# Where matmul operands start: on-chip tiles moved to multiples of 64 and 512 bytes in a fused mixer and FFN block

## The chip, the cores and the metric

The kernel runs on 1 core of one Trainium2 chip. The metric is device time in microseconds (us): the median of repeated executions of the whole program, and for the profile the span from the first to the last instruction of one profiled execution. TensorE (PE) multiplies, VectorE (DVE) and ScalarE (ACT) work on elements, GpSimd (POOL) fills and issues some of the DMAs, SyncE (SP) issues the others. The memory on the core that the engines read has 128 partitions; every tile occupies the same byte range of each partition, and in this text "start" is the byte at which that range begins.

## What is computed

One layer of a block over 1024 tokens of width 1024, all in float32:

```
h = rmsnorm(x);  proj = h @ w_in                      # 5128 columns
q, k, v, f_logit, g_b, g_c, hc, gate_conv, gate_attn = split(proj)
ya = g_b * causal_conv3(g_c * hc)                      # 512 channels, 3 taps
yb = softmax(q k^T / 8 + cumulated log f, causal) v    # 8 heads of 64
merged = sigmoid(gate_conv) * (ya @ w_branch[0]) + sigmoid(gate_attn) * (yb @ w_branch[1])
x = x + rmsnorm(merged @ w_out)
h = rmsnorm(x);  g, u = split(h @ w_gate_up)           # 2816 columns each
x = x + rmsnorm((silu(g) * u) @ w_down)
```

The convolution adds, for each channel, three neighbours in time: `w[2]*z[s] + w[1]*z[s-1] + w[0]*z[s-2]`, with zeros ahead of the first token.

## The kernel before

**Products.** A float32 factor is split into a high and a low part (`split`, L120: a rounding copy on ACT into a tile of type float32r, a subtraction on DVE), and each product is three matmuls (`mm3`, L125): high by high, high by low, low by high. Nearly all of them have 512 columns of the moving tile, 2048 bytes per partition, against a weight tile of 128 columns, 512 bytes. The large products run by a Strassen scheme of seven products of 512 by 512 by 128 in place of eight (`strassen`, L509; `prod`, L485, four times `mm3`).

**Stages, in order.** (1) The first norm, transposes of x against the identity `ident`, and v with the forget logits (`v_tile`, L342): 8 row tiles, each 8 k by 2 halves of 260 columns by 3 matmuls into `pv`, 384 in all; the moving tiles are v's weights `wvh` and `wvl`, [128, 8, 520]. (2) 18 pairs of column blocks of w_in for q and k, the convolution's inputs and the gates: 18 x 7 x 12 = 1512 matmuls into `b1` to `b3`, and `ma`, `mb` for the last pair. The convolution is here: kind "z" (L860) writes the product of two blocks into `zt`, kind "gb" (L866) takes the three taps on DVE. (3) Attention: scores `sp` (pairs of matmuls of 64 rows), transposes `tps`, values `po` in plain float32, and between them the convolution's branch `pba`, 192 matmuls in all. (4) The attention's branch, `pbb`: 192. (5) The output projection `pm`, 384, with the two norms. (6) FFN gate and up, 22 column blocks: 22 x 7 x 12 = 1848, into `b1` to `b3`; the first product of blocks 0 to 6 is made ahead (`f_first`, L1260) while the last rows are normed. (7) The down products `pd`: 7 x 11 x 4 x 3 = 924 (`product`, L1483), then the last norm.

Where `strict` names engines, they keep the order written; elsewhere the order of PE's work is that of the program's scheduler. DMAs are issued by SP (weights, x) and POOL (stores of intermediate results).

**Where tiles lie.** A pool is a stack of tiles that grows from the low end of the memory (left) or from the high end (right); a tile takes its size rounded up to 32 bytes. The left side begins with 1152 bytes of the framework, which is 18 x 64. Then come the constants (L150 to L160): `ident`, `tri`, `ones` and `mask` of 512 bytes, `cw` of 48 (takes 64), `bf` of 32, `ff` of 256, together 2400. So the first pool after them starts at 3552 = 55 x 64 + 32, and since the tiles there are multiples of 64, every tile of the pool `w` (`raw`, `hi`, `lo`, `sx`, `s4`, `s4h`, `s4l`: all weight tiles of stages 2 to 7, and moving tiles of the scores and of `pd`) starts 32 bytes past a multiple of 64; so do `pt`, `ptT`, `yh`, `yl`, `hah`, `hal`, `hch`, `hcl`, `ghi` and `glo` behind it. The right side ends at 229376 = 3584 x 64; the small tiles of `stat` take 1440 bytes, the two tiles of `z` 4128 each (1026 columns are 4104 bytes), so the first tile of `z` starts at 219680 = 3432 x 64 + 32, and below it, in whole multiples of 64, lie `hB11` to `hB22`, `hT12`, `hT34`, `woh`, `wol`, `hth` and `htl`, again 32 past. Exceptions are the second tile of `z` (which serves once as `wbl` and once as `v0`), some of the six `vf` tiles of 2080 bytes, and `ident`: they start at multiples of 64. In `wvh`, 32 past as well, row k starts at 2080 k and its second half 1040 later, so the halves of successive k start 32, 48, 0 and 16 past a multiple of 64. In bytes modulo 512 the places are 480 in the pool `w`, and for `hah`, `hal`, `hch` and `hcl`; 352 for `ptT`, `yh` and `yl`, 160 for `ghi` and `glo`, and 32 for the right side.

The convolution's tile has 1026 columns: two zeros, filled by POOL, and 1024 values, so that each tap reads 512 columns at an offset of 0, 1 or 2.

Of the kernel before, what the change touches and what calls it, by code (L numbers as in the profile page):

```python
# [10 lines left out]
F32 = mybir.dt.float32  # L11
F32R = mybir.dt.float32r
AF = mybir.ActivationFunctionType
ALU = mybir.AluOpType
# [3 lines left out]
P = 128  # L18
S = 1024
D = 1024  # L20
KT = D // P
ST = S // P
NC = 512
H = 8
# [10 lines left out]
C_GB, C_GC, C_HC = 1544, 2056, 2568  # L35
C_GATE_C, C_GATE_A = 3080, 4104
VF = AW + H
TAIL = 4
NPRE = 7

# [5 lines left out]
def block_kernel(  # L46
# [16 lines left out]
    n1, n2 = slice(0, NC), slice(NC, S)  # L63
# [3 lines left out]
    class InOrder:  # L67
# [15 lines left out]
    nc = SimpleNamespace(  # L83
        **{e: InOrder(e) for e in engines}
    )
# [19 lines left out]
    def f32(ap):  # L105
        return ap.bitcast(F32)
# [4 lines left out]
    def sub(o, a, b):  # L111
        nc.vector.tensor_tensor(o, a, b, op=ALU.subtract)

    def mul(o, a, b):
        nc.vector.tensor_tensor(o, a, b, op=ALU.mult)

    def copy(o, a):
        nc.scalar.activation(o, a, AF.Copy)
# [13 lines left out]

    cpool, _ = pool("const")
    stat, _ = pool("stat", 4, side="right")
    dpool, _ = pool("dram", space=DRAM)

    c_dram = dpool.tile([H, S], F32, name="c_dram")
# [9 lines left out]
    ri_dram = [dpool.tile([2, S], F32, name=f"ri_dram{j}") for j in range(4)]  # L147
    sg_dram = [dpool.tile([2, P, S], F32, name=f"sg_dram{d}") for d in range(8)]

    ident = cpool.tile([P, P], F32, name="ident")  # L150
    make_identity(bass_nc, ident)
    tri = cpool.tile([P, P], F32, name="tri")
# [1 line left out]
    ones = cpool.tile([P, P], F32, name="ones")  # L154
    nc.vector.memset(ones, 1.0)
    mask = cpool.tile([P, P], F32, name="mask")
    cw = cpool.tile([P, 3, 4], F32, name="cw")
    bf = cpool.tile([P, H], F32, name="bf")
    nc.gpsimd.dma_start(bf, b_f[0].partition_broadcast(P))
    ff = cpool.tile([P, ST, H], F32, name="ff")  # L160

    def bcast_row(row, p, **kw):
        g = p.tile([P, row.shape[-1]], F32, **kw)
# [27 lines left out]
    zp, z_close = pool("z", side="right")  # L191

    def z_tile(name, dt=F32, w=S):
        return zp.tile([P, S + 2], dt, tag="z", name=name, bufs=2)[:, :w]

    h_pool, h_close = pool("h1", side="right")
    def h_pair(name, shape):
# [6 lines left out]
    hB22 = h_pair("hB22", [P, 4, NC])  # L204
    ax, ax_close = pool("ax", side="right")
    ap, ap_close = pool("a")
    av, av_close = pool("av")
    psa, psa_close = pool("psa", 4, space=PSUM)

# [5 lines left out]
    wrs = []  # L215

    def vf_tile(tag="vf", dt=F32):
        return ap.tile([P, VF], dt, tag=tag, name=tag, bufs=6)

    def load_wv():  # L220
        k = len(wrs)
        wr = ax.tile([P, VF], F32, tag="wr", name="wr", bufs=4) if k < 4 else vf_tile()
        nc.sync.dma_start(wr, win[k * P : (k + 1) * P, C_V : C_V + VF])
        wrs.append(wr)
# [10 lines left out]
    xq.append(load_x(2))  # L235
    warm = st_tile("warm")
    nc.scalar.activation(warm, ones[:, 0:1], AF.Sqrt)
    wvh = av.tile([P, KT, VF], F32R, name="wvh")
    wvl = av.tile([P, KT, VF], F32R, name="wvl")
    gm = ax.tile([P, D], F32, name="gm")  # L240


# [12 lines left out]
    turns(14)  # L255

    def split_wv(k, halves="hl"):
        if "h" in halves:
            copy(wvh[:, k, :], wrs[k])
        if "l" in halves:  # L260
            sub(wvl[:, k, :], wrs[k], f32(wvh[:, k, :]))

    def norm_sum(st):

# [76 lines left out]

    def v_tile(st, ops):  # L342
        pv = psa.tile([P, 2, NC], F32, tag="pv", name="pv", bufs=2)
        hv = VF // 2
        for k in range(KT):
            src = ops[k // 4]
            for n in range(2):
                cs = slice(n * hv, (n + 1) * hv)
                mm3(
                    pv[:, n, :hv],  # L350
                    (src[0][:, k % 4, :], src[1][:, k % 4, :]),
                    (wvh[:, k, cs], wvl[:, k, cs]),
                    k == 0,
                    k == KT - 1,
                )
        vs = av.tile([P, VF], F32, tag="vs", name="vs", bufs=2)
        copy(vs.rearrange("p (n c) -> p n c", n=2), pv[:, :, :hv])
        nc.gpsimd.dma_start(v_dram[st * P : (st + 1) * P, :], vs[:, :AW])
        add(ff[:, st, :], vs[:, AW:VF], bf)

# [186 lines left out]
    t0_, t0_close = pool("att0")  # L547
# [67 lines left out]
    cbs, qks, stacks, vs_, rsums = {}, {}, {}, {}, {}  # L615
# [150 lines left out]
    def step_qk(t):  # L766
        j, rows_ = steps[t]
        if j not in rsums:
            rsums[j] = t0_.tile([P, 2 * ST], F32, tag="rsum", name="rsum", bufs=2)
        for i in rows_:  # L770
            sps[t, i] = qk(j, i)

# [53 lines left out]
    for ij, (kind, j, _, _) in enumerate(jobs):  # L826
        if ij == 2:
            logf_pre = forget_sums()
        if ij == 4:
            forget_store(*logf_pre)  # L830
        if ij < 2:
            if ij == 0:
                heads = [
                    prep_first(wcols(a), t) for (_, _, a, _), t in zip(jobs, ((r0, h0, l0), None))
                ]
                firsts = [strassen_first(w, h1b, psm, pp) for w, _ in heads]
            (w, r1), (c11, p1) = heads[ij], firsts[ij]
            w = {**w, **prep_rest(wcols(jobs[ij][3]), r1)}
            if ij == 1:
                pairs.q.append(pairs.prep(*pairs.srcs.popleft()))  # L840
            _, c12, c21, c22 = strassen(w, h1b, psm, pp, p1)
        elif ij < len(jobs) - 1:
            if ij == 12:
                k_load(0)
                q_load(0)
                cb_of(0, 0)
                cb_of(0, 1)
            c11, c12, c21, c22 = strassen(pairs.get(), h1b, psm, pp)
        else:
            w = pairs.get()  # L850
            psm_close()
            strict[0] = engines
            pss, pss_close = pool("pss", space=PSUM)
            c11, c12, c21, c22 = last_pair(w)
        if kind == "qk":
            so = pp.tile([P, NC], F32, tag="so", name="so")
            copy(so, c11)
            for r, c, t in ((0, n1, so), (0, n2, c12), (1, n1, c21), (1, n2, c22)):
                nc.gpsimd.dma_start(qk_dram[j][r, :, c], t)
        elif kind == "z":  # L860
            zt = z_tile("zt", w=S + 2)
            nc.gpsimd.memset(zt[:, 0:2], 0.0)
            mul(zt[:, 2 : 2 + NC], c21, c11)
            mul(zt[:, 2 + NC : 2 + S], c12, c22)
            zts[j] = zt
        elif kind == "gb":  # L866
            for m, parts in ((j, (c11, c12)), (j + 1, (c21, c22))):
                zt = zts.pop(m)
                for n in range(2):
                    o = n * NC  # L870
                    ot = pp.tile([P, NC], F32, tag="so", name="ot")
                    nc.vector.tensor_scalar(
                        ot, zt[:, o + 2 : o + 2 + NC], cw[:, 2, m : m + 1], None, op0=ALU.mult
                    )
                    for t in (1, 0):
                        nc.vector.scalar_tensor_tensor(
                            ot, zt[:, o + t : o + t + NC], cw[:, t, m : m + 1], ot,
                            op0=ALU.mult, op1=ALU.add,
                        )
                    mul(ot, ot, parts[n])  # L880
                    nc.gpsimd.dma_start(ya_dram[m][:, o : o + NC], ot)
        else:
            so = c11
            strict[0] = ()
            if ij < len(jobs) - 1:
                so = pp.tile([P, NC], F32, tag="so", name="so")
                nc.scalar.activation(so, c11, AF.Sigmoid)
                for t in (c12, c21, c22):
                    nc.scalar.activation(t, t, AF.Sigmoid)
            for r, c, t in ((0, n1, so), (0, n2, c12), (1, n1, c21), (1, n2, c22)):  # L890
                nc.gpsimd.dma_start(sg_dram[j][r, :, c], t)
# [280 lines left out]
    for n in range(2):  # L1172
        ns = slice(n * NC, (n + 1) * NC)
        for d in range(KT):
# [14 lines left out]
            if n == 0:  # L1189
                wr = flat(raw_t())  # L1190
# [185 lines left out]
    count = {"raw": 0, "ops": 1}  # L1376
    SETS = TAIL

# [127 lines left out]
    p1, c22, c11, c12 = (quarter(s_) for s_ in (4, 6, 0, 2))  # L1506

    def wide(name, w=4):
        return gp.tile([P, w], F32, name=name)

    sums = {n: wide(f"sum_{n}") for n in ("c11", "c12", "c22", "c21", "both", "rest")}

    def sq_scale(o, c, key, sl):

# [59 lines left out]
    product(xb, False, to(c22, add, c22, xb), between=rows_0)  # L1574
    product(xb, False, last, TAIL, rows_1)
    gp_close()
# [38 lines left out]
```

## Time and profile before

| what | value |
|---|---|
| time, median of 3 runs | 1361.17 us (1360.53 to 1362.53) |
| the profiled execution: span | 1362.4 us (its own time is not given apart from the span) |
| granted TensorE clock, mean | 0.998 |
| instructions | 17714 |
| DMA | 186.36 MB, 137 GB/s on average |

The page gives the busy time of each engine and its share of the span. Busy time of PE counts from a matmul's start to its modelled end, and matmuls overlap in the pipeline, so how fast PE goes is read from the distance between the starts of successive matmuls: in the list of instructions in order of time, or from a run of matmuls in the chain of waits, its length divided by its count. PEld is the loading of a matmul's weights, which runs beside the matmul before it. All matmuls stand at line 75 of the kernel, a helper that issues every instruction; they are told apart by the names of their tiles, written as out<-moving,weights, with buffer numbers left out (`b` for `b1` to `b3`).

### The profile page before, as it was taken

The numbers are of one execution on the slowest core, as the hardware profiler recorded it, in microseconds if no ns is written. First come the engines' busy times: TensorE is split into PE (matmuls) and PEld (weight loads), VectorE is DVE, ScalarE is ACT, GpSimd is POOL, SyncE is SP. The second block draws the span as 40 slices with busy tenths as digits, with TensorE's granted clock in tenths as the row PEclk, the third lists the DMA queues.
The fourth block names the chain that finished last, engine by engine and source line by source line (L and its number), as shares of the span: only waits on it lengthen the run. The fifth ranks groups of instructions, "written<-read, shape, count | busy, mean of one in ns | idle before, by whom it ended". The sixth has DMA issues, their size and how long they took to land.

```text
span 1362.4 us, 17714 instructions
## 1 busy us (share of the span) xinstructions
PE 1341.2 (98%) x6753; PEld 1099.8 (81%) x6753; DVE 933.0 (68%) x1445; ACT 535.5 (39%) x851; POOL 128.0 (9%) x256
## 2 busy tenths in 40 slices
PE   9999999999999999999999999999999999999997
PEld 7978888888887878788887788888888888888886
DVE  6974767754446766765668698676677766676585
ACT  6642222243345756514446232223222323444452
POOL 0001000010112212000002121100111011000000
PEclk9999999999999999999999999999999999999999
DMA  5432422333325545362235565322333236976441
GB/s 187 117 108 85 125 70 85 102 117 106 99 92 173 156 140 187 114 204 80 90 110 179 162 200 161 101 94 84 116 101 116 86 116 227 355 239 199 161 162 63
DMA packets 153256, 186.36 MB, mean 137 GB/s; under 512 B 9409, under 2 KB 106753, under 8 KB 153170
## 3 DMA queue, kind: packets, MB, share of 16 engines
q1 hardware_dynamic: 138434, 136.67, 32.5%
q0 software_dynamic: 14736, 48.54, 9.7%
q8 instruction: 53, 0.87, 0.3%
q14 instruction: 33, 0.27, 0.1%
HBM read 136.10 MB, written 49.09 MB: 136 GB/s over the span
## 4 chain that ended last, share of the span: by engine, by line
PE 58%; DVE 2%; issue 1%; DMA 1%; ACT 1%; POOL 0%; DVEq 0%; POOLq 0%; ACTq 0%
PE b L75 28%; PE pd L75 16%; PE pm L75 5%; PE pbb L75 3%; PE pba L75 2%; PE po L75 1%; PE tps L75 1%; PE sp L75 1%; DMA pre_dram<-s 1%; DVE tt L75 0%; DMA pre_dram<-c 0%; PE tp L75 0%; ACT tt L75 0%; DVE lo L75 0%; DMA raw<-in_w_gate_up_dram 0%
## 5 line engine op out<-in xcount | busy, mean ns | idle before, releaser
L75 DVE TENSOR_TENSOR c<-c,b 128x512 f32<-128x512 f32 x195 | 133.1, 683 | 93.2 <-PE b L75 68.3
L75 DVE TENSOR_TENSOR lo<-raw,hi 128x1024 fp32r<-128x1024 f32 (+1 forms) x93 | 112.1, 1205 | 86.0 <-PE b L75 71.5
L75 ACT ACTIVATE hi<-raw 128x1024 fp32r<-128x1024 f32 (+1 forms) x100 | 101.7, 1018 | 130.4 <-PE b L75 81.2
L75 PE MATMUL b<-hth,hi 128*128 128x512 f32 x352 | 139.1, 395 | 0.1
L75 PE MATMUL b<-hth,lo 128*128 128x512 f32 x352 | 138.1, 392 | 0.0
L75 PE MATMUL b<-htl,hi 128*128 128x512 f32 x352 | 137.2, 390 | 0.0
L75 ACT ACTIVATE hi<-sx 128x1024 fp32r<-128x1024 f32 x41 | 43.5, 1061 | 222.7 <-PE b L75 197.1
L75 PEld LDWEIGHTS b<-hth,lo 128*128 128x128 f32 x352 | 66.0, 188 | 15.6
L75 PEld LDWEIGHTS b<-hth,hi 128*128 128x128 f32 x352 | 66.1, 188 | 14.8 <-DVE c L75 1.0
L75 PEld LDWEIGHTS b<-htl,hi 128*128 128x128 f32 x352 | 66.1, 188 | 14.6
L75 DVE TENSOR_TENSOR lo<-sx,hi 128x1024 fp32r<-128x1024 f32 x41 | 50.2, 1225 | 34.6 <-PE b L75 30.8
L75 PE MATMUL b<-hah,hi 128*128 128x512 f32 x176 | 70.5, 403 | 2.1 <-ACT c L75 2.1
L75 DVE TENSOR_TENSOR sx<-raw 128x512 f32<-128x512 f32 x78 | 53.7, 688 | 23.4 <-DMA raw<-in_w_in_dram 11.7
L75 PE MATMUL b<-hah,lo 128*128 128x512 f32 x176 | 69.4, 395 | 0.0
L75 PE MATMUL b<-hal,hi 128*128 128x512 f32 x176 | 69.1, 393 | 0.0
L75 PE MATMUL pd<-hi,lo 128*128 128x512 f32 x160 | 62.6, 391 | 0.0
L75 PE MATMUL pd<-hi 128*128 128x512 f32 x160 | 62.3, 392 | 0.0
L75 PE MATMUL pd<-glo,ghi 128*128 128x512 f32 x148 | 57.7, 390 | 0.0
L75 PE MATMUL pd<-ghi 128*128 128x512 f32 x148 | 57.7, 390 | 0.0
L75 PE MATMUL pd<-ghi,glo 128*128 128x512 f32 x148 | 57.6, 389 | 0.0
L75 PE MATMUL b<-hT34h,lo 128*128 128x512 f32 x136 | 53.4, 393 | 0.0
L75 PE MATMUL b<-hT34h,hi 128*128 128x512 f32 x136 | 53.0, 390 | 0.4 <-DVE c L75 0.4
(369 smaller groups left out, 3367.8 us busy)
## 6 DMA issues: line engine op xcount, KB each, us to landing
raw<-in_w_gate_up_dram SPq DMA_DIRECT2D x51, 512.0 KB, 4.0
raw<-in_w_in_dram SPq DMA_DIRECT2D x35, 512.0 KB, 4.2
a_dramS<-um POOLq DMA_DIRECT2D x44, 256.0 KB, 3.1
a_dramA<-um POOLq DMA_DIRECT2D x33, 256.0 KB, 3.0
xt<-in_x_dram SPq DMA_DIRECT2D x16, 512.0 KB, 4.3
sg<-sg_dram SPq DMA_DIRECT2D x32, 256.0 KB, 4.1
graw<-a_dramS SPq DMA_DIRECT2D x14, 512.0 KB, 4.0
sg_dram<-c POOLq DMA_DIRECT2D x24, 256.0 KB, 2.3
```

What stands on the lines that cost most here:

```text
L75: ins = getattr(self.engine, name)(*args, **kw)
```

## The change

It alters where tiles start, and the shape of three tiles. The constants `cw`, `bf` and `ff` come first, with `cw` and `bf` taking 64 bytes each; empty tiles named "pad" are put into the pools `stat`, `a` and `g`; `vf`, `vs` and `rsum` get longer rows; `wvh` and `wvl` hold each half of 260 columns in a row of 272; `zt` has 1024 columns and no zeros, and the taps that would read before the first token leave out the first one or two columns of the first half. Everything computed stays the same.

```diff
+HV = VF // 2
     stat, _ = pool("stat", 4, side="right")
+    stat.tile([P, 24], F32, name="pad", bufs=1)
...
+    cw = cpool.tile([P, 4, 4], F32, name="cw")[:, :3, :]
+    bf = cpool.tile([P, 2 * H], F32, name="bf")[:, :H]
+    ff = cpool.tile([P, ST, H], F32, name="ff")
     ident = cpool.tile([P, P], F32, name="ident")
...
     mask = cpool.tile([P, P], F32, name="mask")
-    cw = cpool.tile([P, 3, 4], F32, name="cw")
-    bf = cpool.tile([P, H], F32, name="bf")
     nc.gpsimd.dma_start(bf, b_f[0].partition_broadcast(P))
-    ff = cpool.tile([P, ST, H], F32, name="ff")
...
-        return zp.tile([P, S + 2], dt, tag="z", name=name, bufs=2)[:, :w]
+        return zp.tile([P, S], dt, tag="z", name=name, bufs=2)[:, :w]
...
     ap, ap_close = pool("a")
+    ap.tile([P, 32], F32, name="pad")
...
-        return ap.tile([P, VF], dt, tag=tag, name=tag, bufs=6)
+        return ap.tile([P, VF + 8], dt, tag=tag, name=tag, bufs=6)[:, :VF]
...
-    wvh = av.tile([P, KT, VF], F32R, name="wvh")
-    wvl = av.tile([P, KT, VF], F32R, name="wvl")
+    wvh, wvl = (
+        av.tile([P, KT, 2, HV + 12], F32R, name=n)[:, :, :, :HV] for n in ("wvh", "wvl")
+    )
...
     def split_wv(k, halves="hl"):
+        wr = wrs[k].rearrange("p (n c) -> p n c", n=2)
         if "h" in halves:
-            copy(wvh[:, k, :], wrs[k])
+            copy(wvh[:, k], wr)
         if "l" in halves:
-            sub(wvl[:, k, :], wrs[k], f32(wvh[:, k, :]))
+            sub(wvl[:, k], wr, f32(wvh[:, k]))
...
-                    (wvh[:, k, cs], wvl[:, k, cs]),
+                    (wvh[:, k, n, :], wvl[:, k, n, :]),
...
-        vs = av.tile([P, VF], F32, tag="vs", name="vs", bufs=2)
+        vs = av.tile([P, VF + 8], F32, tag="vs", name="vs", bufs=2)[:, :VF]
...
-            rsums[j] = t0_.tile([P, 2 * ST], F32, tag="rsum", name="rsum", bufs=2)
+            rsums[j] = t0_.tile([P, 4 * ST], F32, tag="rsum", name="rsum", bufs=2)[:, : 2 * ST]
...
-            zt = z_tile("zt", w=S + 2)
-            nc.gpsimd.memset(zt[:, 0:2], 0.0)
-            mul(zt[:, 2 : 2 + NC], c21, c11)
-            mul(zt[:, 2 + NC : 2 + S], c12, c22)
+            zt = z_tile("zt")
+            mul(zt[:, n1], c21, c11)
+            mul(zt[:, n2], c12, c22)
...
-                        ot, zt[:, o + 2 : o + 2 + NC], cw[:, 2, m : m + 1], None, op0=ALU.mult
+                        ot, zt[:, o : o + NC], cw[:, 2, m : m + 1], None, op0=ALU.mult
                     )
                     for t in (1, 0):
+                        back = 2 - t
+                        skip = 0 if n else back
                         nc.vector.scalar_tensor_tensor(
-                            ot, zt[:, o + t : o + t + NC], cw[:, t, m : m + 1], ot,
+                            ot[:, skip:], zt[:, o + skip - back : o + NC - back],
+                            cw[:, t, m : m + 1], ot[:, skip:],
                             op0=ALU.mult, op1=ALU.add,
                         )
...
     sums = {n: wide(f"sum_{n}") for n in ("c11", "c12", "c22", "c21", "both", "rest")}
+    wide("pad", 80)
```

By the sizes in the new code the constants end at 3584 = 7 x 512, `stat` takes 1536 bytes, the `vf` tiles with their pad 12800 = 25 x 512, the small tiles of the attention's first pool (`cs_`, `cT`, `rsum`) 1024, and the sums with their pad 512. The tiles of 512-column matmuls then start at multiples of 512, v's weight halves, `vf`, and the tiles of the transposes at multiples of 64.

More of the change, by code (lines that the diff above doesn't have):

```diff
@@ L343, in v_tile @@
         pv = psa.tile([P, 2, NC], F32, tag="pv", name="pv", bufs=2)
-        hv = VF // 2
         for k in range(KT):
@@ L347, in v_tile @@
             for n in range(2):
-                cs = slice(n * hv, (n + 1) * hv)
                 mm3(
-                    pv[:, n, :hv],
+                    pv[:, n, :HV],
                     (src[0][:, k % 4, :], src[1][:, k % 4, :]),
-                    (wvh[:, k, cs], wvl[:, k, cs]),
+                    (wvh[:, k, n, :], wvl[:, k, n, :]),
                     k == 0,
@@ L355, in v_tile @@
                 )
-        vs = av.tile([P, VF], F32, tag="vs", name="vs", bufs=2)
-        copy(vs.rearrange("p (n c) -> p n c", n=2), pv[:, :, :hv])
+        vs = av.tile([P, VF + 8], F32, tag="vs", name="vs", bufs=2)[:, :VF]
+        copy(vs.rearrange("p (n c) -> p n c", n=2), pv[:, :, :HV])
         nc.gpsimd.dma_start(v_dram[st * P : (st + 1) * P, :], vs[:, :AW])
```

## The prediction

> **What bounds the kernel now.** I read the page first, then the chain of work that ended last, then the waits of TensorE (PE), and last the single start times of its matmuls.
>
> ```profile
> span 1362.4 us, 17714 instructions
> PE 1341.2 (98%) x6753; PEld 1099.8 (81%) x6753; DVE 933.0 (68%) x1445; ACT 535.5 (39%) x851; POOL 128.0 (9%) x256
> PEclk9999999999999999999999999999999999999999
> ```
>
> PE is busy for 98% of the span at the full granted clock; no other engine comes over 68%. So the time is the number of matmuls times the distance from one start to the next, plus a few waits. The waits of PE (waiting group, releaser, us in total, times, longest) are small; these are the four longest:
>
> ```profile
> PE b L75 <- ACT c L75: 3.0, 3, 2.1
> PE b L75 <- DVE c L75: 3.0, 3, 2.0
> PE spin L75 <- POOL ident masks.py:199: 1.5, 1, 1.5
> PE sp L75 <- ACT hi L75: 1.3, 1, 1.3
> ```
>
> The distance itself stands in the chain in order of time (start, duration, what). A run of matmuls that nothing interrupts gives it by division.
>
> ```profile
> 559.52 11.15 PE pba L75 x48
> 570.68 44.50 PE pbb L75 x192
> 615.17 21.77 PE pm L75 x95
> 779.45 364.95 PE b L75 x1584
> 1144.40 211.20 PE pd L75 x924
> ```
>
> That is 232.3 ns for a matmul of 512 columns in the branch of the convolution (pba), 231.8 in that of attention (pbb), 229.2 in the output projection (pm), 230.4 in the FFN's gate and up products (b) and 228.6 in the down products (pd). For the products of stage 1 the table by stretches (us, then PE busy and its count) serves:
>
> ```profile
> 84.00:397.00 313.00, 312.61 (x1369) 256.39 (x1368) 190.45 (x271) 92.01 (x117) 27.73 (x54) 1.00 0.33 100
> ```
>
> 313.0 us / 1369 is 228.6 ns. By the loops there are 1512 + 192 + 192 + 384 + 1848 + 924 = 5052 such matmuls (in the order stage 1, pba, pbb, pm, FFN, down). Weighted by these counts the mean distance is 229.6 ns, and together they take 1160 us of the 1362. **A nanosecond per matmul is worth 5 us; nothing else in this change has that weight.** The question is whether the distance depends on where the tiles start.
>
> **What the rows say of start addresses.** By the allocations (worked out in the part on the kernel) nearly every tile that a 512-column matmul reads now starts 32 bytes past a multiple of 64. Such a matmul reads 2048 bytes per partition of its moving tile. If the tile is read in pieces of 64 bytes, that is 33 pieces, the first and last half used; from a multiple of 64 it is 32. The trace has one place where the moving start varies: the two halves of v's weights, 260 columns or 1040 bytes each. wvh starts 32 past a multiple of 64, a k row is 2080 bytes, a half 1040, so the remainder is 32, 48, 0, 16 in turn, three matmuls each. Start times of one such tile (start, duration):
>
> ```profile
> 36.53 0.28 PE L75 MATMUL pv<-wvh,hB11h 128*128 128x260 f32 x1
> ...
> 36.89 0.28 PE L75 MATMUL pv<-wvh,hB11h 128*128 128x260 f32 x1
> ...
> 37.25 0.28 PE L75 MATMUL pv<-wvh,hB11h 128*128 128x260 f32 x1
> ...
> 37.61 0.28 PE L75 MATMUL pv<-wvh,hB11h 128*128 128x260 f32 x1
> ...
> 37.97 0.28 PE L75 MATMUL pv<-wvh,hB11h 128*128 128x260 f32 x1
> ...
> 41.79 0.28 PE L75 MATMUL pv<-wvh,hB21l 128*128 128x260 f32 x1
> ```
>
> Remainders 48, 0, 16, 32: 0.36 us for three each, 120 ns. From 36.53 to 41.79 there are 44 distances, 119.5 ns on average. So the start by itself costs nothing. But 1040 bytes touch 17 pieces of 64 from each of these four starts, so this row can't tell whether the *count* of pieces does. The two lengths together can say a little: (229.6 - 119.5) / (33 - 17) = 6.9 ns per piece. Against full speed: transposes read the identity, which starts at a multiple of 64; po reads ptT, which starts 32 past one.
>
> ```profile
> 537.33 1.04 PE L75 MATMUL tps<-ident,pt 128*128 128x128 f32 x8
> 539.82 1.97 PE L75 MATMUL po<-ptT,v 128*64 128x128 f32 x32
> L75 PE MATMUL tps<-ident,pt 128*128 128x128 f32 x274 | 38.8, 277 | 0.0
> L75 PE MATMUL po<-ptT,v 128*64 128x128 f32 x544 | 35.6, 277 | 0.5 <-DVE ptT L75 0.5
> ```
>
> Take one 277 ns off each run: 8 transposes start 0.76 / 7 = 109 ns apart; 32 records of po, two heads side by side, (1.97 - 0.28) / 31 x 2 = 109 ns a pair. That is 0.85 ns a column, against 229.6 / 512 = 0.45 in the others, so I take plain float32 as two steps a column: 109 / 256 is 0.425 ns a step, 16 columns at one step each are 6.8 ns, 17 and 33 pieces are 116 and 224, which leaves 4 and 6 of the measured 119.5 and 229.6. Without pieces, 260 and 512 columns are 110.5 and 217.6, which leaves 9.0 and 12.0. **An account by pieces leaves the more even remainder** (2 ns apart, not 3): it speaks for 33 pieces, but thinly. Against it: po is as fast as the transposes although its start is off, though at half the reading rate a ninth piece could hide. And weight loads don't care:
>
> ```profile
> L75 PEld LDWEIGHTS pbb<-yh,lo 128*128 128x128 f32 x48 | 9.0, 188 | 2.1
> ...
> L75 PEld LDWEIGHTS pbb<-yh,wbl 128*128 128x128 f32 x16 | 3.0, 188 | 0.7
> ```
>
> wbl is the one weight tile of that stage that starts at a multiple of 64 (128 columns are 8 pieces there and 9 in lo): 188 ns both times, mean duration of one load.
>
> **The change part by part.**
>
> *Where tiles start (the pads, the order of the constants).* No instruction is added or moved. Adding up the sizes in the new code, the constants end at a multiple of 512, and so do stat, the six vf tiles with their pad, the small tiles ahead of the attention's pools and the small sums ahead of ghi and glo; so the moving and weight tiles of all 5052 matmuls start at multiples of 512. The price per matmul isn't shown by any row, so it is bounded. One end is 0: no effect of the start at 260 columns, none on weight loads. The other end is the whole excess over full speed, 229.6 - 217.6 = 12.0 ns. Between them lies one piece of 64 bytes, 6.9 ns. Below nothing there is the spread that addresses make already: 228.6 in one group, 232.3 in another, so a loss of 2.7 ns on the mean can't be excluded. I take the one piece, since it is what the two lengths give. That is 5052 x 6.9 = 34.9 us. The scores (sp) run as pairs of half height; some 120 pairs of 256 columns or more, each with one piece more than needed: 0.8 us. Sum 35.7.
>
> Not all of it reaches the end. From the last stretch of the output projection to the first full FFN product the chain runs through other engines (start, duration, what):
>
> ```profile
> 637.03 1.06 ACT hi L75
> ...
> 745.49 4.32 DMA pre_dram<-s
> ...
> 778.70 0.61 DVE c L75
> ```
>
> Between 637 and 779 us stand about 142 / 0.23 = 617 of the matmuls, worth 4.2 us. PE hardly waits there now (the 3.0 and 3.0 us of the first two waits are mostly here), but what feeds it is nearly late already; I let half of it turn into waits, 2.1 us. In the down products DMA and VectorE have room: their share of the stretch 1146 to 1353 is below.
>
> ```profile
> 1146.00:1353.00 207.00, 207.00 (x908) 169.76 (x907) 143.95 (x171) 91.82 (x127) 2.18 (x4) 1.00 0.62 212
> ```
>
> VectorE is busy 144 of 207 us and the DMA engines 62%, so 3% more pace is covered there. Net: 33.6 us.
>
> *v's weight halves padded to 272 columns.* Every half now starts at a multiple of 64, and still touches 17 pieces: by pieces 0, by the full excess 384 x 9.0 = 3.5 us. I take 0. The splits (copy and sub) now run over two runs of 260 instead of one of 520: the same elements, cost 0 between -0.3 and +0.5 us, the size of the waits PE has on them now (0.5 us on wvl).
>
> *The convolution's tile without zero columns.*
>
> ```profile
> L75 DVE SCALAR_TENSOR_TENSOR ot<-zt,cw,ot x16: 742/744/748, 172.2 to 268.8; 128x512 f32<-128x512 f32 x16
> L75 POOL MEMSET zt<- x4: 100/100/100, 64.9 to 212.2; 128x2 f32 x4
> ```
>
> Four fills of 0.1 us on POOL go; nothing on PE waits for them. Eight of the sixteen taps get one or two columns shorter of 744 ns: under 3 ns each. VectorE is at 190 of 313 us in that stretch (the row of 84 to 397), so 0; were that cover gone, 0.4 us. No wait, DMA or queue entry is added anywhere.
>
> [...]
>
> The span is 1362.4 us; no other time of that execution is given, and the timed runs lie at 1361.17, 1.2 below. 1361.2 - 33.6 = **1328 us**.
>
> **The rivals.** *The start makes no difference.* For: weight loads, the four remainders, po. Against: only the thin arithmetic of the two lengths. The time stays at 1361, or shifts a little as the groups' distances shift with other addresses (within 2 us one way or the other).
>
> *The whole excess goes.* If the excess comes from a misaligned stream and not from one more piece, 12.0 ns go per matmul: 60.6 + 3.5 + 1.4 for the pairs, less 3.7 kept as waits between 637 and 779: 1361.2 - 61.8 = 1299. Against: at remainder 0 the 260-column matmul still has its 9 ns.
>
> *Slower: all streams in step.* Moving tile and next weights are read at the same time, and after the change both start at the same place of 512 bytes, everywhere. If the two reads then meet in the same part of the memory, each matmul takes what the worst group takes now, 232.3: 5052 x 2.7 = 13.6, so 1375. It decides from a mean distance of 230.1 on (half a nanosecond up is 2.5 us). Against: in the down products most weights and moving tiles share their remainder of 512 already, and that group is among the fastest (228.6); for: pba and pbb, with other places, are the slowest, so places matter.
>
> *It doesn't do what it says*: some pool ends elsewhere and tiles stay off. My addition of the sizes speaks against it; the time would be 1361.
>
> **How the numbers follow.** One piece less 0.40 (1328); the whole excess 0.15 (1299); no difference 0.24, of which 0.15 within 0.2%, 0.05 faster by a little, 0.04 slower by a little; in step 0.19 (1375, from 1364 up); not done 0.02. What a measurement of this kernel can tell from no change is about 0.2%, 2.7 us. Faster 0.40 + 0.15 + 0.05 = 0.60; same 0.15 + 0.02 = 0.17; slower 0.04 + 0.19 = 0.23. The range must hold the full excess below and the unchanged rate with half of the slower case above: 1292 to 1370. Without the case in step the likeliest sign, faster, has 1292 to 1357.
>
> **What would show it.** In the profile after: the FFN's run of 1584 at 354 us (223.5 ns each) and the down products' 924 at 205; v's matmuls still 120 ns apart; weight loads still 188 ns. A run of 1584 at 365 means that starts don't matter; at 346, that the whole excess was theirs; above 368, that the streams meet. If the distances shrink as said but the span doesn't, the wait must stand in PE's waits between 637 and 779. I am wrong in the step from 33 to 32 pieces if the distance moves and v's moves with it.

## The result, and the profile after

| | before | after |
|---|---|---|
| time, median of 4 runs | 1361.85 us (1360.53 to 1363.19) | 1350.01 us (1349.58 to 1353.05) |
| ratio | | 0.9919 [0.9905, 0.9933] |
| profiled execution: span | 1362.4 us | 1348.2 us (its own time 1350.04 us) |

The change makes the kernel faster by 11.8 us, about a third of the 33.6 us that were predicted; the time lies inside the predicted range, which also held the unchanged time. The executions on record whose span is given take 1.7 to 2.0 us more than their span, so the profiled execution of before took about 1364.2 us (an estimate): of the 14.2 us between the two spans some 2.4 belong to that execution and not to the change. The head of the page of the changed kernel (PE's busy time, share of the span and instruction count first):

```profile
span 1348.2 us, 17709 instructions
PE 1328.5 (99%) x6753; PEld 1098.9 (82%) x6753; DVE 932.3 (69%) x1445; ACT 535.2 (40%) x851; POOL 127.2 (9%) x252
```

PE issues the same 6753 matmuls and still bounds the kernel. The chain of waits of the changed kernel, in order of time (start, us, what), has the runs that the prediction divided:

```profile
556.69 10.90 PE pba L76 x48
567.59 43.52 PE pbb L76 x192
611.11 21.55 PE pm L76 x95
...
771.64 354.18 PE b L76 x1560
...
1137.72 203.67 PE pd L76 x896
```

Length by count: 227.1, 226.7, 226.8, 227.0 and 227.3 ns, where before had 232.3, 231.8, 229.2, 230.4 and 228.6. For stage 1, the table by stretches (us, then PE busy and its count):

```profile
84.00:397.00 313.00, 312.61 (x1382) 258.74 (x1381) 191.83 (x273) 94.12 (x119) 27.89 (x53) 1.00 0.33 101
```

The same 313 us hold 1382 matmuls in place of 1369: 226.5 ns each in place of 228.6. **Five groups that ran at different paces now run at one.** Single start times say the same: before, distances of 226, 229, 231 and 232 ns are all frequent; after, 4675 of 4980 are 226 or 227.

Summing the distances of starts by stage (waits inside included, worked out from the single start times of both traces, in us):

| stage | before | after |
|---|---|---|
| stage 1 products (1428 into `b`) | 328.6 | 325.6 |
| pba | 46.2 | 45.7 |
| pbb | 44.5 | 43.5 |
| pm | 89.1 | 88.6 |
| FFN (1848) | 433.6 | 425.0 |
| pd | 210.9 | 209.9 |
| v (pv) | 50.1 | 50.3 |

Scores, transposes and po are unchanged to 0.1 us. Of the 8.6 us of the FFN some 2.7 are shorter waits; among the kernels below, whatever their pace, these differ by 2 us, so they are not laid to the change. The two longest waits of PE in the changed kernel (waiting group, releaser, us, times, longest) were 3.0 and 3.0 before:

```profile
PE b L76 <- DVE c L76: 2.5, 3, 1.5
PE b L76 <- ACT c L76: 2.1, 3, 1.2
```

What the prediction said would not move did not move. The matmuls of v in the list of single instructions (start, duration), first and last of one tile:

```profile
36.62 0.28 PE L76 MATMUL pv<-wvl,hB11h 128*128 128x260 f32 x1
...
42.15 0.28 PE L76 MATMUL pv<-wvh,hB21l 128*128 128x260 f32 x1
```

5.53 us for 46 distances are 120.2 ns, 119.5 before. Weight loads, in the groups (busy us, mean ns), still take 188 ns:

```profile
L76 PEld LDWEIGHTS pbb<-yh,lo 128*128 128x128 f32 x48 | 9.0, 188 | 1.9
```

So the distance of 512-column matmuls fell with the new starts, but by 2.5 ns, not 6.9. The experiments ask on what exactly.

### The profile page after: what moved, and what is told of

Read it like the earlier page. It is cut to its first block, busy times and chain, and to the rows that moved or that the text cites. A ratio compares the mean times of both kernels' runs of the same rounds, so it can differ in the third digit from the quotient of the medians.

```text
span 1348.2 us, 17709 instructions
## 1 busy us (share of the span) xinstructions
PE 1328.5 (99%) x6753; PEld 1098.9 (82%) x6753; DVE 932.3 (69%) x1445; ACT 535.2 (40%) x851; POOL 127.2 (9%) x252
## 4 chain that ended last, share of the span: by engine, by line
PE 58%; DVE 3%; DMA 2%; issue 1%; ACT 1%; POOL 0%; DVEq 0%; SPq 0%; POOLq 0%; ACTq 0%
PE b L76 28%; PE pd L76 15%; PE pm L76 5%; PE pbb L76 3%; PE pba L76 2%; PE po L76 1%; PE tps L76 1%; PE sp L76 1%; DMA pre_dram<-s 1%; DMA tk<-in_w_down_dram 1%; DVE tt L76 0%; DVE lo L76 0%; PE tp L76 0%; DMA pre_dram<-c 0%; ACT tt L76 0%
## 5 line engine op out<-in xcount | busy, mean ns | idle before, releaser
L76 ACT ACTIVATE hi<-sx 128x1024 fp32r<-128x1024 f32 x41 | 43.5, 1062 | 220.9 <-PE b L76 195.3
L76 DVE TENSOR_TENSOR lo<-sx,hi 128x1024 fp32r<-128x1024 f32 x41 | 50.2, 1224 | 33.6 <-PE b L76 31.4
```

Source lines behind the costliest of these rows:

```text
L76: ins = getattr(self.engine, name)(*args, **kw)
```

## The experiments

The starting theory was that of the prediction (pieces of 64 bytes: what counts is whether the moving tile starts at a multiple of 64). Its rival: what counts is where moving and weight tile start **relative to each other**, since before the change most pairs stood 64 bytes apart modulo 256 (moving 32, weights 480 modulo 512) and after it 0.

**e1: starts by themselves.** Behind the kernel's last store stand runs of 48 matmuls of 512 columns (in some runs fewer columns), with nothing else running. The letters of a name are the starts of moving tile (m) and weights (w) past a multiple of 512: a, b, c, d are 0, 32, 64, 96; q is 16. The runs whose names begin with n have 260 columns.

```diff
+    def probe(name, n, m, w):
+        m, w = m // 4, w // 4
+        ps = psq.tile([P, NC], F32, tag="pr", name=name)
+        for r in range(4):
+            for k in range(4):
+                mm3(
+                    ps[:, :n],
+                    (wh[:, k, w : w + P], wl[:, k, w : w + P]),
+                    (mh[:, k, m : m + n], ml[:, k, m : m + n]),
+                    r == 0 and k == 0, r == 3 and k == 3,
+                )
```

> The changed kernel with an appendix after its last store: runs of 48 matmuls in the kernel's own pattern (high by high, high by low, low by high, four blocks of k), whose moving tile and weight tile start 0, 32, 64 or 96 bytes past a multiple of 512, all 16 combinations at 512 columns, two runs at 16 bytes and one at 48, and runs of 260, 256, 480 and 384 columns. The results of the appendix are not used. Theory 'moving': the distance of starts is 226.7 ns wherever the moving tile is at 0 or 64, and 229 to 232 where it is at 32 or 96, whatever the weights do. Theory 'weights': the same with the weights' start. Theory 'meeting': only combinations in which the two differ modulo 64 (or only those in which both are off) are longer. Theory 'whole lines', the one of the prediction: 32 and 96 cost one piece, 6.9 ns, more than 0 and 64; it needs 233 against 226.7, and 260 columns at 0 and at 32 equal at 120. By columns, 480 at 0 lies 32 x 0.42 = 13 ns below 512, and the excess over 0.42 ns a column is the same 13 ns at 256, 384, 480 and 512 if it is a fixed cost of each matmul.

Some of the runs in the chain of this kernel (start, us, what):

```profile
1365.51 11.19 PE mawbx L77 x48
...
1410.34 10.89 PE mbwbx L77 x48
...
1443.61 11.00 PE mcwax L77 x48
...
1465.82 10.89 PE mcwcx L77 x48
...
1521.28 10.89 PE mdwdx L77 x48
...
1543.29 10.89 PE mawqx L77 x48
...
1565.38 5.70 PE nawax L77 x48
1571.07 5.76 PE nbwax L77 x48
...
1610.04 8.35 PE qawax L77 x48
```

**Pieces are refuted by one row**: in mbwbx both tiles start 32 past a multiple of 64, so the moving tile touches 33 pieces, and it is as fast (10.89 us, 226.9 ns each) as mcwcx with 32. Whenever the two starts are equal, 10.89; apart by 32, 11.19 (233.1 ns); moving 64 ahead of the weights, 11.00 (229.2 ns); weights 16 ahead, 10.89 again, moving tile 16 ahead 11.12 (231.7 ns). With 260 columns the whole effect is 0.06 us in 48, 1.2 ns each; with 256 columns it has the other sign (5.74 us level, 5.66 with the moving tile 32 ahead). No other engine works during these runs, and the only DMAs are some ten packets that fetch instructions, so the loss is not contention with VectorE, ScalarE or DMAs. The first run (46 records in 13.03 us) came after an idle stretch of PE and is left aside.

**e2, e3, e4: the changed kernel with its starts moved apart.** In e2 the left side moves up by 96 bytes, in e3 the right side down by 32, in e4 left up and right down by 64; all three go back to the short `rsum` as well, so that the small tiles fit; pba and nearly all of pbb stand 128 apart again by that.

```diff
     mask = cpool.tile([P, P], F32, name="mask")
+    cpool.tile([P, 24], F32, name="shift")
...
-            rsums[j] = t0_.tile([P, 4 * ST], F32, tag="rsum", name="rsum", bufs=2)[:, : 2 * ST]
+            rsums[j] = t0_.tile([P, 2 * ST], F32, tag="rsum", name="rsum", bufs=2)
```

> The changed kernel with all tiles of the left side moved up by 96 bytes, the right side as changed. 2940 of the 512-column matmuls (stage 1, output projection, the hth products) then have weights at 96 past a multiple of 128 and the moving tile at 0; 2144 (hah and hch products, down products, the branches) have both at 96. Theory 'weights': all matmuls lose the gain, the distance is 229 to 232 everywhere and the time about 1361. Theory 'moving': only the 2144 lose it, about 2.8 ns each or 6 us, so 1356, and stage 1 stays at 226.8. Theory 'meeting': the 2940 lose it, the 2144 keep it: about 1358.

```diff
-    stat.tile([P, 24], F32, name="pad", bufs=1)
+    stat.tile([P, 32], F32, name="pad", bufs=1)
...
-            rsums[j] = t0_.tile([P, 4 * ST], F32, tag="rsum", name="rsum", bufs=2)[:, : 2 * ST]
+            rsums[j] = t0_.tile([P, 2 * ST], F32, tag="rsum", name="rsum", bufs=2)
```

> The changed kernel with all tiles of the right side moved down by 32 bytes, the left side as changed. 2940 of the 512-column matmuls have the moving tile at 96 past a multiple of 128 and the weights at 0; 2148 have both at 0. Theory 'moving': stage 1, the output projection and the hth products go to 229 to 232, the down products stay at 226.8, time about 1358. Theory 'weights': nothing changes, 1350. Theory 'meeting': as 'moving'; it differs from it in the run with the left side moved.

```diff
-    stat.tile([P, 24], F32, name="pad", bufs=1)
+    stat.tile([P, 40], F32, name="pad", bufs=1)
...
     mask = cpool.tile([P, P], F32, name="mask")
+    cpool.tile([P, 16], F32, name="shift")
...
-            rsums[j] = t0_.tile([P, 4 * ST], F32, tag="rsum", name="rsum", bufs=2)[:, : 2 * ST]
+            rsums[j] = t0_.tile([P, 2 * ST], F32, tag="rsum", name="rsum", bufs=2)
```

> The changed kernel with both sides moved by 64 bytes, so that nearly all operands of 512-column matmuls start 64 past a multiple of 128. If multiples of 64 are what counts, the distance stays at 226.8 and the time at 1350. If multiples of 128 or 512 are needed, the distances go to 229 to 232 and the time to about 1361.

All three are slower than the kernel before: e2 1372.36 us, ratio 1.0075 [1.0058, 1.0092]; e3 1370.85 us, 1.0064 [1.0049, 1.0079]; e4 1368.9 us, 1.005 [1.0035, 1.0065]. The expectation of e4 was wrong in its premise: the sides grow towards each other, so moving both by 64 puts them 128 apart (moving 448, weights 64 modulo 512). That makes it the sharpest of the three, since there the main tiles of the 512-column products **do start at multiples of 64, and the kernel is slower than before**. Chain of e4:

```profile
784.42 366.22 PE b L76 x1584
...
1150.64 209.79 PE pd L76 x924
```

FFN, where in 1056 of 1848 matmuls a moving tile of the right side meets weights of the left, 231.2 ns; the down products, whose tiles all lie on the left, 227.1. Stage 1 of e2, whose moving tiles lie on the right and weights on the left, by stretches:

```profile
84.00:397.00 313.00, 312.61 (x1337) 251.23 (x1336) 187.09 (x267) 87.12 (x110) 25.58 (x48) 1.00 0.33 99
```

234.1 ns against 226.5 in the changed kernel: 1337 matmuls in the time of 1382.

**e5, e6: the kernel before with pads alone.** e5 adds 64 bytes on the right and nothing else; e6 adds to that the longer `rsum` and the pad behind the sums. Constants, convolution and v stay as they were, and the tiles of the big products start at 480 modulo 512, 32 past a multiple of 64.

```diff
     stat, _ = pool("stat", 4, side="right")
+    stat.tile([P, 16], F32, name="pad", bufs=1)
```

> The kernel before with one empty tile of 64 bytes added on the right side and nothing else: hB, hT, hth, htl, woh and wol then start at 480 modulo 512 like the weights; no operand of stage 1, the output projection, the gate and up products starts at a multiple of 64. Theory 'equal starts' (what counts is the difference between the start of the moving tile and that of the weights loaded beside it, modulo 512; 0 is the best): 226.8 ns in those stages, pba and pbb still 232, the down products 228: about 3 us less in stage 1, 6 to 8 in the FFN, 0.5 to 1 in the output projection, so 1351 to 1353 (ratio 0.992 to 0.994). Theory 'alignment' (a start at a multiple of 64 is what counts): no gain, 1362, ratio 1.000.

```diff
     stat, _ = pool("stat", 4, side="right")
+    stat.tile([P, 16], F32, name="pad", bufs=1)
...
-            rsums[j] = t0_.tile([P, 2 * ST], F32, tag="rsum", name="rsum", bufs=2)
+            rsums[j] = t0_.tile([P, 4 * ST], F32, tag="rsum", name="rsum", bufs=2)[:, : 2 * ST]
...
     sums = {n: wide(f"sum_{n}") for n in ("c11", "c12", "c22", "c21", "both", "rest")}
+    wide("pad", 80)
```

> The kernel before with three pads only (64 bytes on the right side, rsum of 128 bytes, 320 bytes behind the sums), so that nearly all operands of 512-column matmuls start at 480 modulo 512, none at a multiple of 64. Theory 'equal starts': 226.8 everywhere but in pba, the whole gain of the change: 1350, ratio 0.991 to 0.993, the same as the change. Theory 'alignment': 1362, ratio 1.000.

e5: 1354.25 us, ratio 0.9947 [0.9932, 0.9961]. e6: 1351.26 us, 0.9927 [0.9914, 0.994]. Chain of e5:

```profile
567.80 44.73 PE pbb L75 x192
...
773.33 354.20 PE b L75 x1560
...
1139.52 204.92 PE pd L75 x896
```

Chain of e6:

```profile
567.57 43.84 PE pbb L75 x192
...
772.43 354.19 PE b L75 x1560
...
1138.57 203.71 PE pd L75 x896
```

One pad of 64 bytes gives the FFN its 227.1 ns, and about two thirds of the gain (7.7 of 11.8 us); pbb (`yh` against the weights, 128 apart modulo 256) and pd (`ghi` and `glo` at 160, the other tiles at 480, and 72 of 924 with the moving tile at 160 and the weights at 480) wait for the other two pads, which bring 233.0 to 228.3 and 228.7 to 227.4. **With three pads nearly the whole gain is there, and none of it needs a multiple of 64.**

**e7, e10: the parts that were costed at nothing.** e7 is the changed kernel with the old convolution (zero columns, four fills, full taps; `stat`'s pad shortened so that the rest stays in place), e10 the changed kernel with v's halves unpadded.

```diff
-    stat.tile([P, 24], F32, name="pad", bufs=1)
+    stat.tile([P, 8], F32, name="pad", bufs=1)
...
-            zt = z_tile("zt")
-            mul(zt[:, n1], c21, c11)
-            mul(zt[:, n2], c12, c22)
+            zt = z_tile("zt", w=S + 2)
+            nc.gpsimd.memset(zt[:, 0:2], 0.0)
+            mul(zt[:, 2 : 2 + NC], c21, c11)
+            mul(zt[:, 2 + NC : 2 + S], c12, c22)
...
```

> The changed kernel with the convolution of before (two zero columns, filled by POOL, full taps); the pad on the right is cut so that all other tiles lie as in the change. Theory 'the convolution's edit is free': the change's time, 1350, within 0.2%. Rival: it holds a part of the gain, up to 0.4 us of fills and taps; more than 1 us would surprise.

```diff
-        av.tile([P, KT, 2, HV + 12], F32R, name=n)[:, :, :, :HV] for n in ("wvh", "wvl")
+        av.tile([P, KT, 2, HV], F32R, name=n) for n in ("wvh", "wvl")
```

> The changed kernel with v's weight halves not padded (260 columns each, as before). Theory 'equal starts': the 260-column matmuls of v go from 120.2 to about 119.6 ns, as before the change; 384 x 0.6 = 0.2 us, so the time stays at 1350, ratio 0.991 to 0.993. Rival: the padding holds a part of the gain, 1 us or more slower without it.

e7: 1350.13 us, 0.9915 [0.9902, 0.9928]. e10: 1350.39 us, 0.9913 [0.9899, 0.9926]. Both equal the changed kernel. v's matmuls in e10 stand 119.9 ns apart on average, 120.2 after: the padding buys nothing. The run of down products in e7 has the count of before, so that the two compare without division (211.20 us before):

```profile
1131.61 209.79 PE pd L76 x924
```

**e8: with what period.** The kernel of e1 with other runs: weights at 0 and moving tile at 0 to 480 in steps of 32 (dax to dpx), small differences around an equal start of 64 (ebx +4, eex -16), and fewer columns at equal starts (fax 512, fbx 496, fdx 320).

```diff
-RUNS = [('mawax', 512, 0, 0), ('mawbx', 512, 0, 32),
+RUNS = [('dax', 512, 0, 0), ('dbx', 512, 32, 0), ('dcx', 512, 64, 0),
...
```

> The changed kernel with an appendix as in the first probe: 48 matmuls of 512 columns at each difference of starts 0, 32, 64 to 480 (weights at 0), at differences of -4, 4, 8, -8, -16, -24 and -32 bytes around 0, and runs of 512, 496, 448, 320, 384 and 260 columns. Theory 'equal starts modulo 512': 226.7 at 0 alone, about 229 at 64, 233 at 32, 96, 416, 448 and 480 as in the first probe, 229 to 233 at the others; nothing below 226. If the period were 128 or 256, then 128, 256 and 384 (or 256) would give 226.7 as well. The in-kernel groups say 231 to 233 at 288 and 384 and 229 at 192. By columns: 0.417 ns each on a fixed 13 ns.

From its chain:

```profile
1376.27 11.00 PE dcx L77 x48
...
1398.48 11.20 PE dex L77 x48
...
1443.30 10.88 PE dix L77 x48
...
1465.39 11.00 PE dkx L77 x48
...
1543.32 11.36 PE ebx L77 x48
...
1576.92 10.88 PE eex L77 x48
...
1610.20 10.89 PE fax L77 x48
...
1641.38 7.04 PE fdx L77 x48
...
1659.41 8.32 PE ffx L77 x48
```

**256 bytes apart (dix) is as good as 0, 320 (dkx) is as 64 (dcx), 128 (dex) is bad**: the period is 256. The other twelve multiples of 32 take 11.19 to 11.24 us. 192 was expected at about 229 ns and has 233: a miss. The moving tile 4 bytes ahead (ebx) is the worst of all, 236.7 ns; 16 bytes behind (eex) costs nothing. Between and around these it is not a smooth curve: 4 behind costs nothing, while 8 behind has 230.0 ns, 24 behind and 8 ahead 233.3. From 320 to 512 columns the time rises from 146.7 to 226.9 ns: 0.418 ns a column, and 226.9 less 512 of these leaves 13 ns that no start tried here removes. Level runs of other lengths lie within 3.4 ns of that line; the 480 columns of e1, 216.9 ns, are 10 ns below its level 512, where 13 were expected. At 384 columns a moving tile 64 ahead (ffx) is no slower than a level one (qawax of e1, 8.35 us).

**e11: the period in the kernel.** The changed kernel with the right side lower by 256 bytes (`cT` lies in another pool to make room).

```diff
-    stat.tile([P, 24], F32, name="pad", bufs=1)
+    stat.tile([P, 88], F32, name="pad", bufs=1)
...
-cT = t0_.tile([H * ST, P], F32, name="cT")
+cT = pp.tile([P, NC], F32, tag="so", name="cT")[: H * ST, :P]
```

> The changed kernel with the right side moved down by 256 bytes (a small tile of the forget gates, cT, is taken from another pool to make room): in 2940 of the 512-column matmuls the moving tile starts 256 bytes away from the weights modulo 512, in the others they are equal. Theory 'equal starts modulo 256', from the second probe (226.65 ns at 256): 226.8 everywhere, time 1350, ratio 0.991 to 0.993. Theory 'modulo 512': the 2940 lose 2 to 7 ns each, 1356 to 1370.

1350.28 us, ratio 0.9917 [0.9904, 0.9931], and its chain has the FFN of the changed kernel:

```profile
772.45 354.17 PE b L76 x1560
```

**e9, e12: which weights meet the moving tile.** While a matmul streams, the next one's weights are loaded: in the changed kernel a matmul starts at 999.85 us, the load of the next one's weights at 999.86, 0.19 us long, and that next matmul at 1000.08. Does the moving tile's start count against its own weights or against the next ones? The two can be told apart where high and low parts start differently. In e9 one part is shifted by 32: gbx both low parts, gcx the low moving tile, gdx the low weights, gex the high moving tile; ggx is the even case. The runs hax to hdx are in bfloat16, with differences of 0, 32, 64 and 0 bytes.

```diff
+RUNS = [('gax', 512, (0, 0), (0, 0), 0), ('gbx', 512, (0, 32), (0, 32), 0), ('gcx', 512, (0, 32), (0, 0), 0), ('gdx', 512, (0, 0), (0, 32), 0), ('gex', 512, (32, 0), (0, 0), 0),
...
+                    (h[:, k, w : w + P], l[:, k, w2 : w2 + P]),
+                    (a[:, k, m : m + n], b[:, k, m2 : m2 + n]),
```

> The changed kernel with an appendix as in the probes, the order of each three being moving high with weights high, moving low with weights high, moving high with weights low. It tells which weights a moving tile's start is to be compared with: its own, or those of the next matmul, which are loaded beside it. gbx has both low tiles at 32 and both high ones at 0. Theory 'next weights': every matmul then has the difference 0 to the weights loaded beside it, 226.7 ns, 10.9 us for 48. Theory 'own weights': two of three differ by 32, (226.7 + 2 x 233.3) / 3 = 231, 11.1 us. gcx has the low moving tile alone at 32, gdx the low weights alone: one of three differs by either theory, 229. In gex the high moving tile alone is at 32: two of three, 231. The runs hax to hdx are bfloat16, 512 columns, differences 0, 32, 64 and 0 bytes: if the effect is one of the reading rate, bfloat16, with half the bytes, shows none, the same distance in all four, and below 226.7.

From the chain of e9:

```profile
1365.74 11.14 PE gbx L77 x48
1376.88 11.12 PE gcx L77 x48
1388.01 11.19 PE gdx L77 x48
1399.19 11.10 PE gex L77 x48
...
1420.67 0.65 PE hbx L77 x3
...
1431.03 1.08 PE hcx L77 x5
...
1441.39 1.51 PE hdx L77 x7
...
1451.75 11.01 PE gfx L77 x48
...
```

Neither theory fits. In gcx and gdx one matmul in three is off by either of them, which should give about 229 ns; the runs have 231.7 and 233.1. And gbx, 226.7 by 'next weights' and 231 by 'own weights', has 232.1. In bfloat16 the runs begin 10.36 us apart whatever the starts: 215.8 ns each, no effect (a few of their records are missing, so the counts in the rows aren't used).

e12 takes shifts that cost nothing, or little, when all matmuls have them: 256 on one part (kbx, kcx) or on both low parts (kdx), -16 on the low moving tile (kex), 64 on the low moving tile, the low weights or both (kfx, kgx, khx).

```diff
+RUNS = [('kax', 512, (0, 0), (0, 0), 0), ('kbx', 512, (0, 256), (0, 0), 0), ('kcx', 512, (0, 0), (0, 256), 0), ('kdx', 512, (0, 256), (0, 256), 0), ('kex', 512, (64, 48), (64, 64), 0),
...
```

> The changed kernel with a last appendix on mixed starts, order as in the third probe. kbx: the low moving tile alone at 256; kcx: the low weights alone at 256; kdx: both; with a period of 256 all are as kax and kix, 226.7 ns. kex: the low moving tile alone 16 bytes lower than the rest; by the second probe (226.67 at -16 for all three) 226.7, if a mix of two good differences is good. kfx, kgx, khx: low moving tile, low weights, or both, 64 higher than the rest. Theory 'next weights' says about 227.4, 227.4 and 226.7, theory 'own weights' 227.4, 227.4 and 228.2; theory 'rhythm' (a run is as slow as if all its matmuls were out of step once some are) says 229 or more in all three.

From the chain of e12:

```profile
1376.52 10.88 PE kcx L77 x48
1387.40 10.88 PE kdx L77 x48
1398.28 11.27 PE kex L77 x48
1409.55 11.15 PE kfx L77 x48
...
1431.78 11.10 PE khx L77 x48
1442.88 10.89 PE kix L77 x48
```

Shifts of 256 mix freely. But -16, free when all have it (eex, 226.7 ns), costs 8 ns a matmul when one in three has it (kex, 234.8: a miss); 64, which gives 229 when all have it, gives 231 to 232 when only some do. Of the three accounts in the expectations only the one by rhythm ("229 or more in all three") is not refuted, and the runs are slower than the 229 ns of a run in which all matmuls stand 64 apart. So a *change* from one matmul to the next seems to cost by itself.

The single start times of the kernels show such a cost. In the FFN of before, 54 groups, nearly all of 12 matmuls with both starts at 480, stand between groups that are 64 apart: the first ten distances of a group average 231.6 ns, the eleventh and twelfth 226.7. In e5, where nothing around them differs, such matmuls run at 227.1 throughout. In e2 and e4, among others that stand 160 or 128 apart, the first three distances average 231.1 and 231.7, the rest 227. In the down products of before, where the place changes from 160 to 480 while both starts stay equal, a typical group begins with 228, 229, 234, 235, 225, 230, 236, 229, 232 and 231 ns and then runs at 227; e6 brings all of them to one place, and the pace is 227 throughout. So after a change, even from level to level, it takes three to ten matmuls until the pace of the new place is reached. A steady mix is not always dearer than its parts, though: where one matmul in three of the down products stands 192 apart (moving 160, weights 480), the distances settle near 229, and (2 x 226.7 + 233.1) / 3 is 228.8. Whether reads meet at all, and why mixes of 32, 64 or -16 cost more than their parts, stays open.

Put together, worked out from single start times and the tiles' addresses (bytes modulo 256; waits left out; the probe's column from e8, once a run has settled):

| moving less weights | kernel, ns | matmuls of | probe, ns |
|---|---|---|---|
| 0 | 226.9 (after), 227.1 (e5) | 4980, 4087 | 226.7 |
| 64 | 229.3 (before) | 2903 | 228.9 |
| 128 | 232.9 (e4) | 3235 | 233.3 |
| 160 | 234.2 (e2) | 2905 | 234.2 |
| 224 | 233.4 (e3) | 2905 | 233.1 |

Most matmuls of the kernel before stood, as it happened, at the second best difference that e8 found among multiples of 32. That is why the way to the best was short.

## Why the prediction was right in sign and wrong in size

- **What bounds the kernel: right.** 5052 matmuls, a nanosecond on each worth 5 us. By the stages' paces the mean distance fell by 2.5 ns, 12.5 us; with the 2.7 us of shorter waits in the FFN that accounts for the 14.2 us between the two spans to within 1 us; the medians lie 11.8 apart, the profiled execution of before being some 2.4 us longer than the median.
- **The failed step: "that is 33 pieces ... from a multiple of 64 it is 32", at 6.9 ns.** The price came from two lengths, (229.6 - 119.5) / (33 - 17), as if all time went in pieces, and was kept because it left even remainders. e1 shows 33 pieces at full pace (mbwbx), e4 shows 32 pieces slower than before, e6 the gain with 33. In its place stands the difference of the two starts modulo 256: from 64 to 0, 2.2 ns in the probe, and 2.5 on the mean of the kernel. The sign came out right by luck: multiples of 512 also made all starts equal, and e4 shows that multiples of 64 without equal starts are slower than the kernel before. The even remainder was thin evidence: the probes' lengths lie up to 3.4 ns off a line of 0.418 ns a column and 13 ns fixed, more than the 1 ns that spoke for pieces.
- **The rival "in step" named the right pair of tiles and had its sign backwards.** It named moving tile and weights and their relative place; equal places are the best (226.7 ns in the probes), and most differing ones the slowest (232 to 234). That the two reads meet in the memory was its assumption, and no run shows it. Its own "against" was the row that mattered: the down products, where most starts were equal, were among the fastest groups, and pba and pbb, with other places, the slowest. Had the groups been ordered by that difference, the gain could have been estimated from the fastest distances already in the trace, 226 to 227 ns: about 2.6 ns, 13 us.
- **"No difference" and "the whole excess"** fall too. e2 to e4, which move the starts and little else, take the changed kernel from 1350.0 us to between 1368.9 and 1372.4, so there is an effect, and by e1 it hangs on two starts together. Of the excess of 12.0 ns over 217.6 no start tried here took more than 2.9: the fastest float32r runs of 512 columns have 226.7 ns. The bfloat16 runs of e9 have 215.8.
- **The waits of 2.1 us kept between 637 and 779: wrong side.** The two longest waits of PE shrank from 6.0 to 4.6 us together. As these waits differ by 2 us among the kernels of the experiments too, the size says little, but none was added.
- **Convolution at 0, v's padding at 0, weight loads at 188 ns, v's matmuls at 120 ns: right** (e7, e10, the rows after). The taps became shorter by a column or two, on an engine that has 191.8 us of work in 313.
- **What would show it:** the FFN's run was to take 354 us for 1584; it took 354.18 for 1560, which is 359.6 for 1584, between the two marks given for "one piece" and "no effect" and nearer to the middle than to either.

## What to carry to other kernels

In float32r products of 512 columns, compare where moving and weight tiles start, modulo 256 bytes (226.7 ns a matmul when equal, 228.9 to 236.7 at most other differences tried), and bring all pairs to the same remainder, and to one place if that is cheap; a pad of 64 bytes in one pool was worth 7.7 us here, while aligning the main tiles to 64 bytes with the sides 128 apart lost 7. Nothing here says that shorter matmuls gain. The pace to look at is the length of an uninterrupted run in the chain divided by its count: groups with different paces in one kernel are a hint that places matter, and here the fastest of their distances gave the gain's size. When a price is taken from two sizes, see first whether a fixed cost per instruction explains them as well.

## What was not expected of the hardware

- Two starts that are each harmless cost up to 10 ns a matmul by their difference: with the moving tile 4 bytes ahead of the weights 236.7 ns, 32 ahead or behind 233, 64 ahead 229, 16 behind, level, or 256 ahead 226.7.
- The difference does best if it stays the same from one matmul to the next: -16 on one matmul in three costs 8 ns on the average of all, on every one nothing. After a change, three (e2, e4) to ten matmuls (the FFN of before) pass before the pace of the new place is reached.
- bfloat16 matmuls show none of it at differences of 0, 32 and 64 bytes (215.8 ns in e9), and weight loads last 188 ns before and after. In e9 the loads last 187 to 189 ns in the slow runs and the level one alike (gdx at 233.1 ns a matmul, ggx at 226.9), but the pace of the float32r matmuls does depend on where those weights start (gdx has the low weights alone 32 further), with no other engine at work. Whether the loading slows the running matmul is not shown by this.
